# Seven half-size block products for eight in both products of an MLP, with weight sums made in DRAM

## The chip, the core and the metric

The kernel runs on one core of a Trainium2 chip. The core has a matrix engine (TensorE, PE in the profile, with PEld for its weight loads), a vector engine (VectorE, DVE), a scalar engine (ScalarE, ACT), GpSimd (POOL) and SyncE (SP). SP and POOL issue the DMAs, each in the order of its own instruction stream, and 16 DMA engines carry them. The metric is the device time of one execution in microseconds (us).

## The reference

One decoder layer in float32 on 1024 tokens of width 1024, cut here to its outline:

```python
n = rms_norm(h, ln_mix_g); proj = n @ w_in                       # q, k, v of two mixers, and gates
ya = dilated_mixture(rope(qa), rope(ka), va) @ w_branch_a        # 12 heads, windows at strides 1, 4, 16
yb = stick_breaking(qb, kb, vb) @ w_branch_b                     # 8 heads
h = h + (sigmoid(ga + b) * ya + sigmoid(gb + b) * yb) @ w_out
h = h + cross_attention(rms_norm(h), rms_norm(mem))              # 256 memory tokens
u = conv3(rms_norm(h, ln_ffn_g) @ w_up) + conv_b                 # w_up 1024 x 5632, causal, per column
h = h + (silu(u[:, :2816]) * u[:, 2816:]) @ w_down               # w_down 2816 x 1024
return rms_norm(h, ln_f_g)
```

## The kernel before

Every matrix product is made of fp32 values split in two: `split` (lines 71 to 74) lets ACT write the rounded high part `wh` and DVE the rest `wl`, and `mm3` (lines 86 to 90) issues three matmuls for each pair of 128x128 and 128x512 blocks. Raw weights come through `raw_w` (line 65, tile `wr`, two buffers), which SP loads.

The program has three parts. **Mixers**: ten pairs of heads, numbered 0 to 9. For a pair, `proj_pair` projects q, k and v (tile `mm`, or `mmv` in `v_group`); `rope` sends four DMAs `xw<-xs` on POOL (line 284) and multiplies on POOL (line 286); `k_stacks` sends the copies `kh` and `kl` on POOL (lines 245, 247); `dil_scores` multiplies q with k into `zs` (lines 254, 255) for the pairs 0 to 5. While one pair is attended, the next one is projected. **Middle**: output projection and cross-attention for two halves of 512 tokens. **MLP**: `up_pair` makes, for one half of the tokens, two gate and two value columns of 128 from eight blocks each (tile `pu`), runs the convolution (ACT line 763, DVE lines 766 and 767), silu and the product (line 770); `down_half` multiplies with w_down through `tok_gemm` (tile `mmt`, left sides `ahl`). Each half takes 44 x 8 x 3 = 1056 matmuls for w_up and 2 x 22 x 4 x 3 = 528 for w_down.

The instructions are not kept in the order in which the Python code issues them. A scheduler places each where its own timeline finds the engine free and the operands there; it keeps the order of dependent instructions only. Each engine then runs its stream in order: an instruction that waits holds up all that stand behind it on that engine, DMA issues included. DMAs of SP share eight semaphores in turn, and so do those of POOL, so that an issue waits until the eighth DMA before it on its queue has landed.

## Time and profile before

| | us |
|---|---|
| median of three runs (1783.76 to 1789.73) | 1786.36 |
| profiled execution, its own time | 1788.84 |
| its span | 1786.8 |
| PE busy in the span | 1751.7 (98%) |
| DVE, ACT, POOL busy | 1076.0, 901.9, 204.5 |
| mean granted TensorE clock | 0.996 |

The profiled execution is 2.5 us slower than the median, and 2.0 us of its time lie outside the span. A matmul of the page lasts some 390 ns from start to modelled end, but the next one starts before it ends; what a matmul costs is read from the spacing of the starts, or from a stretch in which PE does nothing else. A DMA line gives bytes and the busy share of the 16 DMA engines; "to landing" is the time from issue to the last byte.

### The profile page before, as it was taken

The numbers are of one execution on the slowest core, as the hardware profiler recorded it, in microseconds if no ns is written. First come the engines' busy times: TensorE is split into PE (matmuls) and PEld (weight loads), VectorE is DVE, ScalarE is ACT, GpSimd is POOL, SyncE is SP. The second block draws the span as 40 slices with busy tenths as digits, with TensorE's granted clock in tenths as the row PEclk, the third lists the DMA queues.
The fourth block names the chain that finished last, engine by engine and source line by source line (L and its number), as shares of the span: only waits on it lengthen the run. The fifth ranks groups of instructions, "written<-read, shape, count | busy, mean of one in ns | idle before, by whom it ended". The sixth has DMA issues, their size and how long they took to land.

```text
span 1786.8 us, 24490 instructions
## 1 busy us (share of the span) xinstructions
PE 1751.7 (98%) x8974; PEld 1441.6 (81%) x8974; DVE 1076.0 (60%) x1970; ACT 901.9 (50%) x1772; POOL 204.5 (11%) x376
## 2 busy tenths in 40 slices
...
GB/s 292 142 122 96 82 95 85 92 59 108 137 48 101 54 77 77 191 169 247 130 83 72 82 72 83 95 101 100 95 95 95 143 103 97 94 95 94 99 101 84
DMA packets 58681, 191.52 MB, mean 107 GB/s; under 512 B 10176, under 2 KB 10432, under 8 KB 58560
## 3 DMA queue, kind: packets, MB, share of 16 engines
...
## 4 chain that ended last, share of the span: by engine, by line
PE 78%; issue 11%; DMA 4%; DVE 4%; POOL 1%; ACT 1%; SPq 0%; POOLq 0%; DVEq 0%; ACTq 0%
PE pu L89 9%; PE pu L88 9%; PE pu L90 9%; PE mmt L88 7%; PE mmt L89 7%; PE mmt L90 7%; PE mm L89 4%; PE mm L88 4%; PE mm L90 4%; DMA xw<-xs 2%; PE avs L493 1%; PE mmv L88 1%; PE mmv L90 1%; PE mmv L89 1%; PE tra L486 1%
## 5 line engine op out<-in xcount | busy, mean ns | idle before, releaser
L73 DVE TENSOR_TENSOR wl<-wr,wh 128x512 fp32r<-128x512 f32 x464 | 328.3, 710 | 352.1 <-ACT wh L72 350.7
L72 ACT ACTIVATE wh<-wr 128x512 fp32r<-128x512 f32 x464 | 289.7, 626 | 468.8 <-PE pu L89 159.2
L90 PE MATMUL pu<-a2h,wl 128*128 128x512 f32 x704 | 274.9, 390 | 0.0
L89 PE MATMUL pu<-a2l,wh 128*128 128x512 f32 x704 | 274.6, 390 | 0.0
L88 PE MATMUL pu<-a2h,wh 128*128 128x512 f32 x704 | 274.4, 390 | 0.0
L88 PE MATMUL mm<-a2h,wh 128*128 128x512 f32 x640 | 253.4, 398 | 7.6 <-ACT a2h L97 7.6
L89 PE MATMUL mm<-a2l,wh 128*128 128x512 f32 x640 | 254.2, 397 | 0.0
L90 PE MATMUL mm<-a2h,wl 128*128 128x512 f32 x640 | 252.8, 397 | 0.0
L88 PEld LDWEIGHTS pu<-a2h,wh 128*128 128x128 f32 x704 | 132.2, 188 | 27.2
L90 PEld LDWEIGHTS pu<-a2h,wl 128*128 128x128 f32 x704 | 132.2, 188 | 27.2
L89 PEld LDWEIGHTS pu<-a2l,wh 128*128 128x128 f32 x704 | 132.2, 188 | 27.0
L88 PEld LDWEIGHTS mm<-a2h,wh 128*128 128x128 f32 x640 | 121.7, 190 | 31.7 <-ACT a2h L97 8.1
L89 PEld LDWEIGHTS mm<-a2l,wh 128*128 128x128 f32 x640 | 121.9, 190 | 24.1 <-issue 1.0
L90 PEld LDWEIGHTS mm<-a2h,wl 128*128 128x128 f32 x640 | 121.3, 190 | 24.6 <-issue 1.4
L89 PE MATMUL mmt<-wl,ahl 128*128 128x512 f32 x352 | 137.7, 393 | 0.0
L90 PE MATMUL mmt<-wh,ahl 128*128 128x512 f32 x352 | 136.3, 389 | 0.0
L88 PE MATMUL mmt<-wh,ahl 128*128 128x512 f32 x352 | 129.5, 392 | 0.0
L479 DVE TENSOR_TENSOR_SCAN kp<-kp 128x128 f32<-128x128 f32 (+7 forms) x64 | 86.8, 1356 | 21.5 <-ACT kp L476 21.4
L766 DVE SCALAR_TENSOR_TENSOR y<-u,vec,y 128x512 f32<-128x512 f32 x88 | 66.1, 751 | 44.0 <-ACT y L763 44.0
L367 ACT ACTIVATE sp<-sp,nm 128x128 f32<-128x128 f32 (+1 forms) x96 | 42.4, 443 | 73.4 <-DVE nm L365 73.3
L88 PEld LDWEIGHTS mmt<-wh,ahl 128*128 128x128 f32 x352 | 66.1, 188 | 15.1
L90 PEld LDWEIGHTS mmt<-wh,ahl 128*128 128x128 f32 x352 | 66.1, 188 | 14.7
...
## 6 DMA issues: line engine op xcount, KB each, us to landing
wr<-in_w_up_dram SPq DMA_DIRECT2D x88, 512.0 KB, 3.3
wr<-in_w_down_dram SPq DMA_DIRECT2D x44, 512.0 KB, 3.3
wr<-in_w_in_dram SPq DMA_DIRECT2D x37, 512.0 KB, 4.0
ga_d<-xr POOLq DMA_DIRECT2D x16, 512.0 KB, 4.4
g<-ga_d SPq DMA_DIRECT2D x16, 512.0 KB, 4.2
wr<-in_w_out_dram SPq DMA_DIRECT2D x16, 512.0 KB, 3.4
wr<-in_w_v_dram SPq DMA_DIRECT2D x12, 512.0 KB, 4.0
...
```

Of the source, the lines that this page charges most:

```text
L72: nc.scalar.activation(hi, raw, AF.Copy)
L73: nc.vector.tensor_tensor(lo, raw, f(hi), op=ALU.subtract)
L88: nc.tensor.matmul(ps, wh, rh, start=first, stop=False)
L89: nc.tensor.matmul(ps, wh, ro, start=False, stop=False)
L90: nc.tensor.matmul(ps, wo, rh, start=False, stop=last)
L367: nc.scalar.activation(sp[:, a, :n], sp[:, a, :n], AF.Exp, scale=0.125, bias=nm[:, a:a + 1], accum_out=ost[:, 130 + a:131 + a])
L479: nc.vector.tensor_tensor_scan(rev, rev, rev, 1.0, op0=ALU.mult, op1=ALU.bypass)
L486: nc.tensor.transpose(tp[:, b * P:(b + 1) * P], gg[:, (b0 + b) * P:(b0 + b + 1) * P], ident)
L493: nc.tensor.matmul(av[a * 64:(a + 1) * 64, (i % 4) * P:(i % 4 + 1) * P], st["v"][:, b, a * 64:(a + 1) * 64], ats[a][b // 4][:, (b % 4) * P ...
L766: nc.vector.scalar_tensor_tensor(y, u[:, 1:HT + 1], vec[:, cw + 1:cw + 2], y, op0=ALU.mult, op1=ALU.add)
```

## The change

Both products of the MLP are written as a 2x2 block product with seven products of blocks instead of eight (Winograd's form of Strassen's scheme). For w_up the token halves are the columns of the right side, the two halves of the 1024 inputs are its rows, and gate and value columns are the two rows of the left side; for w_down the halves are the tokens, the even and odd groups of 128 inner columns, and the two output halves.

The sums and differences that the scheme needs are made as follows. Of the **weights**: in DRAM, in `weight_sums`. For two column groups at a time, it issues four DRAM-to-DRAM copies on SP (lines 517, 518, 520, 522 of the changed file) and three adding DMAs on POOL (519, 521, 523), in a chain of seven steps in which each reads what an earlier one wrote. There are 17 such chains (11 for w_up, 6 for w_down, the last one of half the size), so 68 copies and 51 adding DMAs. `sum_step` advances the chains by one step after each second unit of the pairs 1 to 9. Of the **normalized tokens**: on DVE and ACT, in `right_sums`. Of the **activations**: on DVE, in `up_end`, from where POOL stores seven variants in DRAM (`r_d`); `down` loads them back.

A product accumulates into a PSUM bank that is read, then added to further (`pA`, `pB`, `pD`; `dA`, `dB`). The residual `h` is parked in DRAM during the MLP. For the first six column groups the two products that need only the first half of the tokens are made during cross-attention (`up_early`) and parked in DRAM too. Weights are split in one piece of 1024 columns (two buffers) where it was two of 512 (four buffers). The convolution runs over 1024 columns at a time, without the carried columns between token halves.

The diff, cut to its core ("..." marks what is left out):

```diff
+NEARLY = 6
...
+    su_d = dp.tile([NF, P, 4, HT], F32, name="su_d")
+    sd_d = dp.tile([NF // 2, P, 4, HT], F32, name="sd_d")
+    r_d = dp.tile([NF // 2, 7, P, HT], F32, name="r_d")
+    e_d = dp.tile([NEARLY, 2, P, HT], F32, name="e_d")
+    h_d = dp.tile([8, P, D], F32, name="h_d")
...
-        hi = bp.tile([P, n], F32R, tag="wh", name="wh", bufs=4)
-        lo = bp.tile([P, n], F32R, tag="wl", name="wl", bufs=4)
+        hi = bp.tile([P, n], F32R, tag="wh", name="wh", bufs=2)
+        lo = bp.tile([P, n], F32R, tag="wl", name="wl", bufs=2)
+        return split_to(hi, lo, raw)
+
+    def split_to(hi, lo, raw):
         nc.scalar.activation(hi, raw, AF.Copy)
         nc.vector.tensor_tensor(lo, raw, f(hi), op=ALU.subtract)
         return hi, lo
...
+    def weight_sums(dst, w1, w2):
+        c = slice(0, HT), slice(HT, 2 * HT)
+        add = dict(accum_op=ALU.add)
+        return [
+            lambda: nc.sync.dma_start(dst[:, :, 1], w1[:, :, c[0]]),
+            lambda: nc.sync.dma_start(dst[:, :, 2], w2[:, :, c[0]]),
+            lambda: nc.gpsimd.dma_start(dst[:, :, 1:3].rearrange("g p a c -> g p (a c)"), w2, **add),
+            lambda: nc.sync.dma_start(dst[:, :, 0], dst[:, :, 2]),
+            lambda: nc.gpsimd.dma_start(dst[:, :, 0], w1[:, :, c[0]], **add),
+            lambda: nc.sync.dma_start(dst[:, :, 3], dst[:, :, 0]),
+            lambda: nc.gpsimd.dma_start(dst[:, :, 3], w1[:, :, c[1]], **add),
+        ]
...
+    sums = []
+    for g in range(0, NF, 2):
+        sums.append(weight_sums(su_d[g:g + 2], w_up[g:g + 2], w_up[NF + g:NF + g + 2]))
+    for kg in range(0, NF // 2, 2):
+        e = min(kg + 2, NF // 2)
+        sums.append(weight_sums(sd_d[kg:e], w_down[0, kg:e], w_down[1, kg:e]))
...
+    def sum_step():
+        n = sums_n[0]
+        sums_n[0] += 1
+        for d in range(7):
+            b = n - d
+            if 0 <= b < len(sums):
+                sums[b][d]()
...
             fn(*a)
+            if p and u % 2:
+                sum_step()
...
-    def up_pair(th, fp, acts):
...
-                ps = pp.tile([P, HT], F32, tag="mm", name="pu", bufs=3)
-                feat_gemm(ps, w_up[j], n3[th])
-                u = xp.tile([P, HT + 2], F32, tag="u", name="u", bufs=2)
-                y = xp.tile([P, HT], F32, tag="y", name="y", bufs=4)
...
-                nc.scalar.activation(u[:, 2:], ps, AF.Copy)
-                cw = V_CW + 3 * j
-                nc.scalar.activation(y, ps, AF.Identity, scale=vec[:, cw + 2:cw + 3], bias=vec[:, V_CB + j:V_CB + j + 1])
-                if th == 0:
-                    nc.gpsimd.tensor_copy(carry[:, j], u[:, HT:HT + 2])
-                nc.vector.scalar_tensor_tensor(y, u[:, 1:HT + 1], vec[:, cw + 1:cw + 2], y, op0=ALU.mult, op1=ALU.add)
-                nc.vector.scalar_tensor_tensor(y, u[:, 0:HT], vec[:, cw:cw + 1], y, op0=ALU.mult, op1=ALU.add)
-                ys.append(y)
-            nc.scalar.activation(ys[0], ys[0], AF.Silu)
-            nc.vector.tensor_tensor(a2[:, e], ys[0], ys[1], op=ALU.mult)
-            acts.append(a2[:, e])
...
-    def down_half(th, acts):
...
-        for ch in range(2):
-            tok_gemm(th, ch, NF // 2, w_down, lhs, final)
...
+    def product(ps, w, r, first):
+        for kk in range(4):
+            ks = slice(kk * P, (kk + 1) * P)
+            mm3(ps, (w[0][:, ks], w[1][:, ks]), (r[0][:, kk], r[1][:, kk]), first and kk == 0, kk == 3,
+                skip_group_check=True)
...
+    def up_early(g):
+        l11, l12 = gate_weights(g)
+        pa, pb = bank("mm", 3, "pe"), bank("mm", 3, "pe")
+        p1, c11 = etile("p1"), etile("c11")
+        product(pa, l11, R["11"], True)
+        nc.scalar.activation(p1, pa, AF.Copy)
+        product(pb, l12, R["21"], True)
+        nc.vector.tensor_tensor(c11, pb, p1, op=ALU.add)
+        nc.gpsimd.dma_start(e_d[g, 0], p1)
+        nc.gpsimd.dma_start(e_d[g, 1], c11)
...
+    def right_blocks(xns):
+        hi, lo = act2()
+        R["22"], R["t1"] = (hi[:, 0:4], lo[:, 0:4]), (hi[:, 4:8], lo[:, 4:8])
+        b12 = [htile([P, 2, HT], "hu", "b12") for _ in range(2)]
+        b22 = [htile([P, 2, HT], "hy", "b22") for _ in range(2)]
+        for k in range(4):
...
+                nc.scalar.activation(b[k // 2][:, k % 2], tp, AF.Copy, scale=vec[:, V_FFN + q:V_FFN + q + 1])
+        return b12, b22
+
+    def right_sums(b12, b22):
+        for n in ("t2", "t3", "t4"):
+            R[n] = mp.tile([P, 4, HT], F32R, name=n + "h"), mp.tile([P, 4, HT], F32R, name=n + "l")
+
...
+        t1, t2 = [], []
+        for i in range(2):
+            c = slice(2 * i, 2 * i + 2)
+            a = htile([P, 2, HT], "hr", "t1f")
+            nc.vector.tensor_tensor(a, f(R["11"][0][:, c]), b12[i], op=ALU.subtract)
+            nc.vector.tensor_tensor(a, a, f(R["11"][1][:, c]), op=ALU.add)
+            t1.append(a)
+            b = htile([P, 2, HT], ("hr", "hy")[i], "t2f")
+            nc.vector.scalar_tensor_tensor(b, b22[i], -1.0, a, op0=ALU.mult, op1=ALU.subtract)
+            t2.append(b)
+            put("t2", b, c)
+        for i in range(2):
+            c = slice(2 * i, 2 * i + 2)
+            nc.vector.tensor_tensor(b12[i], b22[i], b12[i], op=ALU.subtract)
+            put("t3", b12[i], c)
+        for i in range(2):
+            put("t1", t1[i], slice(2 * i, 2 * i + 2))
+        for i in range(2):
+            put("22", b22[i], slice(2 * i, 2 * i + 2))
+        for i in range(2):
+            c = slice(2 * i, 2 * i + 2)
+            nc.vector.scalar_tensor_tensor(t2[i], t2[i], -1.0, f(R["21"][0][:, c]), op0=ALU.mult, op1=ALU.subtract)
+            nc.vector.tensor_tensor(t2[i], t2[i], f(R["21"][1][:, c]), op=ALU.subtract)
+            put("t4", t2[i], c)
+
...
+            nc.gpsimd.memset(u[n][:, 0:2], 0.0)
+        u["A"] = bank("zz", 2, "pA")
+        if g < NEARLY:
+            u["p1"] = etile("p1")
+            nc.sync.dma_start(u["p1"], e_d[g, 0])
+            nc.sync.dma_start(u["ug"][:, 2:2 + HT], e_d[g, 1])
         else:
...
+            l11, u["l12"] = gate_weights(g)
+            product(u["A"], l11, R["11"], True)
+            u["p1"] = etile("p1")
+            nc.scalar.activation(u["p1"], u["A"], AF.Copy)
+        return u
+
+    def sum_weights(g, c):
+        raw = htile([P, 2, HT], "hr", "sr")
+        nc.sync.dma_start(raw, su_d[g][:, c:c + 2])
+        hi = mp.tile([P, 2, HT], F32R, tag="mh", name="mh", bufs=2)
+        lo = mp.tile([P, 2, HT], F32R, tag="ml", name="ml", bufs=2)
+        split_to(hi, lo, raw)
+        return [(hi[:, i], lo[:, i]) for i in range(2)]
...
+    def up_middle(g, u):
+        early = g < NEARLY
+        if not early:
+            d = bank("mm", 3, "pD")
+            product(d, u["l12"], R["21"], True)
+            nc.vector.tensor_tensor(u["ug"][:, 2:2 + HT], d, u["p1"], op=ALU.add)
+        s2, s3 = sum_weights(g, 0)
+        product(u["A"], s2, R["t2"], early)
+        u["U2"] = etile("U2")
+        if early:
+            nc.vector.tensor_tensor(u["U2"], u["A"], u["p1"], op=ALU.add)
+        else:
+            nc.scalar.activation(u["U2"], u["A"], AF.Copy)
+        u["B"] = bank("tr", 2, "pB")
+        product(u["B"], s3, R["t3"], True)
+        s1, u["s4"] = sum_weights(g, 2)
+        product(u["A"], s1, R["t1"], False)
+        u4 = etile("U4")
+        if early:
+            nc.vector.tensor_tensor(u4, u["A"], u["p1"], op=ALU.add)
+        else:
+            nc.scalar.activation(u4, u["A"], AF.Copy)
+        nc.vector.tensor_tensor(u["uv"][:, 2 + HT:2 + T], u["B"], u4, op=ALU.add)
+
+    def up_end(g, u):
+        early = g < NEARLY
+        product(u["A"], u["s4"], R["22"], False)
+        c12 = u["ug"][:, 2 + HT:2 + T]
+        if early:
+            nc.vector.tensor_tensor(c12, u["A"], u["p1"], op=ALU.add)
+        else:
+            nc.scalar.activation(c12, u["A"], AF.Copy)
+        raw = bp.tile([P, HT], F32, tag="wr", name="wr", bufs=2)
+        nc.sync.dma_start(raw, w_up[NF + g][:, HT:])
+        product(u["B"], split(raw), R["t4"], False)
+        nc.vector.tensor_tensor(u["uv"][:, 2:2 + HT], u["B"], u["U2"], op=ALU.add)
...
+            nc.scalar.activation(y, x_[:, 2:2 + T], AF.Identity, scale=cw[:, c0 + 2:c0 + 3], bias=vec[:, cb:cb + 1])
+            nc.vector.scalar_tensor_tensor(y, x_[:, 1:1 + T], cw[:, c0 + 1:c0 + 2], y, op0=ALU.mult, op1=ALU.add)
+            nc.vector.scalar_tensor_tensor(y, x_[:, 0:T], cw[:, c0:c0 + 1], y, op0=ALU.mult, op1=ALU.add)
+            if not sign:
+                nc.scalar.activation(y, y, AF.Silu)
+            ys.append(y)
+        a = ys[1]
+        nc.vector.tensor_tensor(a, ys[0], a, op=ALU.mult)
...
+            nc.gpsimd.dma_start(r_d[kg, 0], a[:, :HT])
...
+        nc.vector.tensor_tensor(t[0], r11, r12, op=ALU.subtract)
...
+    def down():
+        KG = NF // 2
+        left = [lambda kg: w_down[0, kg][:, :HT], lambda kg: w_down[0, kg][:, HT:], lambda kg: sd_d[kg][:, 3],
+                lambda kg: w_down[1, kg][:, HT:], lambda kg: sd_d[kg][:, 2], lambda kg: sd_d[kg][:, 0],
+                lambda kg: sd_d[kg][:, 1]]
...
+        def run(ps, i, first):
+            for kg in range(KG):
+                raw = dn.tile([P, 2, HT], F32, tag="rl", name="rl", bufs=6)
+                nc.sync.dma_start(raw[:, 0], r_d[kg, i - 1])
+                nc.sync.dma_start(raw[:, 1], left[i - 1](kg))
+                hi = dn.tile([P, 2, HT], F32R, tag="dh", name="dh", bufs=4)
+                lo = dn.tile([P, 2, HT], F32R, tag="dl", name="dl", bufs=4)
+                split_to(hi, lo, raw)
+                for t in range(4):
+                    ts_ = slice(t * P, (t + 1) * P)
+                    mm3(ps[t], (hi[:, 0, ts_], lo[:, 0, ts_]), (hi[:, 1], lo[:, 1]), first and kg == 0, kg == KG - 1,
+                        skip_group_check=True)
...
+        def into(ps, th, ch, op, last=None):
+            for t in range(4):
+                hs = h[4 * th + t][:, ch * HT:(ch + 1) * HT]
+                nc.vector.tensor_tensor(hs, hs, ps[t], op=op)
+                if last is not None:
+                    square(4 * th + t, ch, dn.tile([P, HT + 4], F32, tag="sq", name="sq", bufs=2)[:, :HT], last)
...
+        run(A, 1, True)
...
+        B = [bank("zz", 2, "dB") for _ in range(2)] + [bank("tr", 2, "dB") for _ in range(2)]
+        run(B, 2, True)
+        into(B, 0, 0, ALU.add, 0)
+        run(A, 6, False)
+        into(A, 0, 1, ALU.subtract)
+        run(B, 7, True)
+        into(B, 1, 1, ALU.subtract)
+        run(A, 5, False)
+        into(A, 1, 1, ALU.subtract, 0)
+        run(B, 4, False)
+        into(B, 0, 1, ALU.subtract, 1)
+        out_half(0)
+        run(A, 3, False)
+        into(A, 1, 0, ALU.add, 1)
+        out_half(1)
...
-    n3 = [norm_T(0, V_FFN, True)]
+    n3 = norm_T(0, V_FFN, True)
+    R["11"], R["21"] = [tuple(x_[:, c:c + 4] for x_ in n3) for c in (0, 4)]
...
-    acts = [[], []]
-    for fp in range(NEARLY + 1):
-        up_pair(0, fp, acts[0])
+    for g in range(NEARLY // 2):
+        up_early(g)
...
-    down_half(0, acts[0])
-    for fp in range(NP_):
-        up_pair(1, fp, acts[1])
-    down_half(1, acts[1])
+    xns = normed(1)
+    for t in range(4, 8):
+        spill_h(t)
+    b12, b22 = right_blocks(xns)
+    for g in range(NEARLY // 2, NEARLY):
+        up_early(g)
...
+    right_sums(b12, b22)
+    before = None
+    for g in range(NF):
+        u = up_start(g)
+        if before is not None:
+            up_end(g - 1, before)
+        up_middle(g, u)
+        before = u
+    up_end(NF - 1, before)
+    ms.close()
+    dn = ctx.enter_context(tc.tile_pool(name="dn", bufs=1, side="right"))
+    down()
```

**SP, the first weight loads.** `wr` are weights for PE, `xk` tokens for the norm, `su_d` and `sd_d` the sums in DRAM, `rs_p` scales. Before, from the second load of `wr` after the tables:

```order
L65 DMA wr<-in_w_v_dram 128x1024
L158 DMA xk<-in_x_dram 128x1024 x3
L65 DMA wr<-in_w_v_dram 128x1024 x2
L175 DMA rs_p_653<-rs_d 128x2x1 x4
L177 DMA rs_p_654<-rs_d 64x8x1 x2
L65 DMA wr<-in_w_in_dram 128x1024 x5
```

Now, the same stretch, from the last but one first step of the chains:

```order
L517 DMA sd_d<-in_w_down_dram 256x512
L518 DMA sd_d<-in_w_down_dram 256x512
L71 DMA wr<-in_w_v_dram 128x1024
L517 DMA sd_d<-in_w_down_dram 128x512
L518 DMA sd_d<-in_w_down_dram 256x512
L518 DMA sd_d<-in_w_down_dram 128x512
L71 DMA wr<-in_w_v_dram 128x1024
L520 DMA su_d<-su_d 256x512
L71 DMA wr<-in_w_in_dram 128x1024
L520 DMA su_d<-su_d 256x512
L71 DMA wr<-in_w_in_dram 128x1024
L520 DMA su_d<-su_d 256x512 x7
```

The third load of `w_v` now stands behind 31 of the 34 copies of the first two steps, and all 68 copies stand ahead of the second pair of tables, where the code issues them between the pairs 1 and 6.

**POOL, the k copies of pair 1.** `xw` is rope's swapped copy, `kh` and `kl` are the stacked k, `o_d` attended tokens. Before:

```order
L284 DMA xw<-xs 32x1024 x4
L245 DMA kh<-kh 64x1024 x2
L247 DMA kl<-kl 64x1024
L286 TENSOR_TENSOR xw<-xw,sin 128x1024
L247 DMA kl<-kl 64x1024
L398 DMA o_d<-ost 128x132
```

Now, up to the last `kl` of pair 1:

```order
L523 DMA su_d<-in_w_up_dram 256x512 x5
L298 TENSOR_TENSOR xw<-xw,sin 128x1024
L523 DMA su_d<-in_w_up_dram 256x512
L523 DMA sd_d<-in_w_down_dram 256x512
L296 DMA xw<-xs 32x1024 x4
L257 DMA kh<-kh 64x1024
L523 DMA sd_d<-in_w_down_dram 256x512
L257 DMA kh<-kh 64x1024
L259 DMA kl<-kl 64x1024
L523 DMA sd_d<-in_w_down_dram 256x512
L259 DMA kl<-kl 64x1024
```

Ahead of that last `kl` stand all 17 adding DMAs of line 519, all 17 of line 521 and 14 of the 17 of line 523, the last step of the chains.

**DVE, the start of the MLP.** `t1f` to `t4l` are the sums of the token blocks and their low parts, `ml` the low part of summed weights, `U` a partial result. Now, ten rows from the preparation (before, DVE has weight splits and the convolution of further column groups here):

```order
L862 TENSOR_TENSOR t1f<-a2h,b_9836 128x1024
L1072 TENSOR_SCALAR ncw<-vec 128x66
L82 TENSOR_TENSOR t3l<-b_9835,t3h 128x1024
L82 TENSOR_TENSOR a2l<-b_9838,a2h 128x1024
L82 TENSOR_TENSOR t2l<-t2f,t2h 128x1024
L863 TENSOR_TENSOR t1f<-t1f,a2l 128x1024
L871 TENSOR_TENSOR b_9836<-b_9838,b_9836 128x1024
L82 TENSOR_TENSOR ml<-sr,mh 128x1024
L879 SCALAR_TENSOR_TENSOR t2f<-t2f,a2h 128x1024
L865 SCALAR_TENSOR_TENSOR t2f<-b_9838,t1f 128x1024
```

New operations of 1024 columns fill DVE between the last transposes and the first complete right side `t2` of a block product.

## Rows read from the trace of the kernel before

**Rows 1.** The page, part 1: busy us (share of the span) and instructions.
```profile
PE 1751.7 (98%) x8974; PEld 1441.6 (81%) x8974; DVE 1076.0 (60%) x1970; ACT 901.9 (50%) x1772; POOL 204.5 (11%) x376
```
**Rows 2.** Timeline of PE: start us, duration us, three matmuls in a row.
```profile
20.19 0.39 PE L89 MATMUL mm<-a2l,wh 128*128 128x512 f32 x1
20.42 0.39 PE L90 MATMUL mm<-a2h,wl 128*128 128x512 f32 x1
20.65 0.39 PE L88 MATMUL mm<-a2h,wh 128*128 128x512 f32 x1
```
**Rows 3.** Busy us by stretch (instructions); then granted clock, DMA share, GB/s.
```profile
25.00:131.00 106.00, 101.90 (x592) 86.93 (x590) 72.40 (x106) 50.10 (x100) 39.54 (x47) 1.00 0.53 148
131.00:735.00 604.00, 593.40 (x3582) 481.64 (x3580) 372.50 (x809) 310.44 (x697) 99.54 (x155) 0.99 0.31 91
1295.00:1420.00 125.00, 125.00 (x548) 102.60 (x547) 67.00 (x114) 55.88 (x107) 4.20 (x6) 1.00 0.31 100
1420.00:1655.00 235.00, 235.00 (x1039) 194.58 (x1038) 137.93 (x201) 121.44 (x201) 21.56 (x43) 1.00 0.32 104
```
**Rows 4.** Groups by line and form on PE: busy us, mean ns, idle before.
```profile
L90 PE MATMUL pu<-a2h,wl 128*128 128x512 f32 x704 | 274.9, 390 | 0.0
L89 PE MATMUL mmt<-wl,ahl 128*128 128x512 f32 x352 | 137.7, 393 | 0.0
```
**Rows 5.** DMAs from 0 to 25 us: GB/s in 40 slices, then the sum.
```profile
GB/s 0 0 27 212 242 226 154 200 252 272 311 279 406 426 419 406 377 397 419 397 420 419 393 406 416 413 413 406 396 388 395 398 423 426 413 426 420 419 420 419
DMA packets 3220, 8.53 MB, mean 341 GB/s; under 512 B 349, under 2 KB 605, under 8 KB 3220
```
**Rows 6.** DMAs from 25 to 131 us: the sum.
```profile
DMA packets 6868, 15.70 MB, mean 148 GB/s; under 512 B 3059, under 2 KB 3059, under 8 KB 6860
```
**Rows 7.** Timeline of SP's DMA issues: start us, duration us, count.
```profile
25.41 0.33 SPq L65 DMA_DIRECT2D wr<-in_w_v_dram  x1
...
41.76 3.86 SPq L65 DMA_DIRECT2D wr<-in_w_v_dram  x2
...
96.20 67.56 SPq L65 DMA_DIRECT2D wr<-in_w_in_dram  x5
```
**Rows 8.** Timeline of POOL, around the k copies of pair 1.
```profile
97.42 1.05 POOL L245 DMA_DIRECT2D kh<-kh  x2
...
106.76 0.56 POOL L247 DMA_DIRECT2D kl<-kl  x1
```
**Rows 9.** Timeline of PE, the first scores of pair 1.
```profile
130.68 0.36 PE L254 MATMUL zs<-kh,qa 128*128 128x256 f32 x1
```
**Rows 10.** Groups by line and form on DVE and ACT: busy us, mean ns.
```profile
L73 DVE TENSOR_TENSOR wl<-wr,wh 128x512 fp32r<-128x512 f32 x456 | 325.2, 715 | 352.0 <-ACT wh L72 350.7 <-PE mm L90 0.6
L767 DVE SCALAR_TENSOR_TENSOR y<-u,vec,y 128x512 f32<-128x512 f32 x88 | 66.2, 752 | 2.9
L548 DVE TENSOR_TENSOR h<-mmt,h 128x512 f32<-128x512 f32 x48 | 32.6, 686 | 14.3 <-PE mmt L90 14.2
L580 DVE TENSOR_TENSOR yl<-wr,yh 128x1024 fp32r<-128x1024 f32 x6 | 7.3, 1225 | 15.0 <-ACT yh L579 14.8
L579 ACT ACTIVATE yh<-wr 128x1024 fp32r<-128x1024 f32 x6 | 6.4, 1060 | 16.7 <-DMA wr<-yt_d 16.7
L763 ACT ACTIVATE y<-pu,vec 128x512 f32<-128x512 f32 x88 | 68.0, 772 | 0.0
L761 ACT ACTIVATE u<-pu 128x512 f32<-128x512 f32 x88 | 51.2, 582 | 0.0
```
**Rows 11.** DMA issues by line: count, KB each, median us to landing.
```profile
wr<-in_w_up_dram SPq DMA_DIRECT2D x88, 512.0 KB, 3.3
o_d<-ost POOLq DMA_DIRECT2D x32, 33.0 KB, 1.8
```

171 lines of the change are left out of this document (111 added, 60 removed).

## The prediction

> **What bounds the kernel now.** The page's first part shows PE busy for 98% of the span, DVE for 60% and ACT for 50% [rows 1]. Durations on PE mislead: the timeline shows matmuls of 0.39 us that start 0.227 us apart [rows 2], so neighbours overlap. The price of a matmul is the spacing. The table by stretch says it for the MLP: in the stretch from 1295 to 1420 us, when w_down is multiplied, 548 matmuls take 125 us (0.228 us each), and from 1420 to 1655 us, w_up for the second half, 1039 take 235 us (0.226), both at a granted clock of 1.00 with DVE at 54 to 59% [rows 3]. So the MLP is paced by PE, and each matmul taken away there is worth 0.227 us, not the 390 ns of the grouped rows [rows 4]. The mixers are paced by PE too, but by a small margin: from 25 to 131 us PE is busy 102 of 106 us, and there POOL and the DMA engines (0.53) are busiest [rows 3]. Two more things are to be seen in the early stretch: SP issues the weights just ahead of their use (two at 41.8 us, five from 96 to 164 us) [rows 7], and POOL sends the k of pair 1 at 97 to 107 us [rows 8] for scores that start at 130.7 us [rows 9]. Nothing there has slack beyond some 25 us.
>
> **What the change removes.** The w_up product has 3 x 704 = 2112 matmuls, the w_down product 3 x 352 = 1056 [rows 4]. Seven instead of eight block products take an eighth away: 264 + 132 = 396. At 0.227 us that is **-90 us**, all on the path, as nothing else ends there.
>
> **What it adds in the MLP.** A 1024-column TENSOR_TENSOR takes DVE 1.225 us, a 512-column one out of PSUM 0.686; a SCALAR_TENSOR_TENSOR of 512 takes 0.752, so at most 1.5 for 1024 [rows 10]. `right_sums` is 18 plain and 4 three-operand operations of 1024: 18 x 1.225 + 4 x 1.5 = 28 us. A column group g below 6 needs, on DVE, five additions out of PSUM (3.4), two splits of summed weights (2.5) and half a split (0.7), four convolution steps (6.0), the product (1.2) and on average two differences (1.4): 15.2 us, while its five block products of 12 matmuls give PE 5 x 12 x 0.227 = 13.6 us. For the six groups DVE needs 28 + 91 = 119 us and PE 82. Of the 37 us, the last convolution and product (9 us) need not be done before PE goes on, and some 3 us of sums run beside the last transposes: **+25 us**, between 5 (`up_early` covers more of the sums) and 40 (none of it is covered). From group 6 on DVE has 15 us, ACT some 11 (three splits at 1.06, one at 0.6, four copies at 0.58, two convolution starts of at most 1.54 and silu) and PE 7 x 12 x 0.227 = 19 us: covered. In `down`, each step has 12 matmuls (2.7 us) against one split of 1.06 on ACT and 1.225 on DVE: covered; if that cover were gone, it would be 0 to 1 us for each of 77 steps. The pools are changed twice; the first change lies under the sums, the second exposes a load, a high part and a low part: 3.3 [rows 11] + 1.06 + 1.2 = **+6 us** (0 to 12). Last results and the longer final multiplications: **+4 us** (0 to 8). The MLP as a whole: -90 + 25 + 6 + 4 = **-55 us** (-85 to -30). The parked tiles, the r_d stores and loads and the wider weight splits lie beside PE work of 14 to 19 us a group and go at nothing; without that cover they cost a load each, 3.3 us.
>
> **What the sums move: the queues.** This decides the sign. The scheduler has pulled the 68 copies and 51 adding DMAs to the first place where SP and POOL are free. On SP, the third weight load of `w_v` stands behind 31 copies; on POOL, the rope and k copies stand among the adding DMAs. Both engines issue in order, and each issue waits for the eighth one before it, so SP and POOL go on at the pace at which the DMA engines carry the sums. The last point that holds PE is the last `kl` of pair 1 on POOL. Ahead of it are adding DMAs of 17.3 MB (step 3), 8.65 MB (step 5) and 14 x 0.52 = 7.3 MB (step 7), and, as each step needs the one before, copies of 17.3 + 8.65 + 7.3 MB: 33.3 MB copied and 33.3 MB added. Behind it waits `zs` of pair 1 on PE, and behind that the whole program. In the kernel before, that matmul starts at 131 us [rows 9]; by then 8.5 MB had moved by 25 us [rows 5] and 15.7 MB from 25 to 131 us [rows 6]. The sums begin at about 25 us, when SP has issued its second `w_v` load [rows 7].
>
> How fast? No row shows a DRAM-to-DRAM copy or an adding DMA. The nearest is the stretch 0 to 25 us, with loads queued up without a gap: slices of 390 to 426 GB/s [rows 5], I take 420. A load touches DRAM once per byte. A copy there touches it twice; an addition reads two operands and writes one, three times. The bounds are to count every byte once (15.7 + 66.6 = 82 MB, 196 us, the point at 221 us) and every touch (15.7 + 2 x 33.3 + 3 x 33.3 = 182 MB, 434 us, the point at 459 us). I take the upper one, since both ends of these transfers lie in the place that the 420 GB/s came from. The delay is then 459 - 131 = **+328 us**. What PE does before that point it did before, too, so the wait is not won back: afterwards PE has 593 us of work in 604 [rows 3].
>
> The Trainium skill ("DMA: Bandwidth & Descriptors", section "Latency and other measured facts") gives 207 to 214 GB/s for copies between HBM tensors; by it the 33.3 MB of copies alone would take some 159 us, an estimate, which is also what two touches at 420 GB/s give, and no run here shows it yet.
>
> **Sum.** 1788.8 for the profiled execution, + 328 - 55 = 2062; less the 2.5 us by which that execution is above the median: **2059 us**.
>
> **Rivals.**
> *Reads set the pace.* A copy counts once, an addition twice (two reads), writes run beside: 15.7 + 33.3 + 66.6 = 115.6 MB at 420 GB/s, 275 us; the point at 300 us, delay 169, time 1900. For it speaks that a load is also a read with a write (into SBUF) that costs no extra at 420 GB/s [rows 5]; against it, that here the writes go to DRAM as well. The Trainium skill ("Collectives: The Full Stack", section "The bandwidth ceiling: the fold count and why AG ≠ RS ≠ AR") has a reduction run at half a copy's rate because it reads two sources; that is this case, and no row here shows it.
> *Every byte counts once.* The point at 221 us, delay 90, time 1786 + 90 - 55 = 1821. Against it speaks that an addition must read its target.
> *The sums hide beside the mixers, faster.* Over 25 to 735 us the DMA engines are busy a third of the time [rows 3], so there is room for 66.6 MB twice over if the queues let other work pass. Then only the MLP counts: 1786 - 55 = 1731. It decides below a delay of 55 us: the point must be reached by 186 us, 82 MB in 161 us, 511 GB/s. The trace has no slice above 426.
> *Rows go out one by one.* If an adding DMA carries one row at a time on each engine and each takes the 1.8 us of the smallest stores [rows 11]: 4224 + 4224 + 3584 rows over 16 engines, 752 in turn, 1354 us; time about 3000. For it: the additions read, add and write back the same place. Against it: nothing in the trace shows such a lack of overlap.
>
> **How the numbers follow.** All touches 0.50; reads only 0.25; bytes once 0.08; hidden 0.07; row by row 0.10. The likeliest gives 2059. The range takes in the first three cases: from 1815 up to 2059 plus 25 for a poorer MLP and 95 for a rate that is a fifth lower over the 434 us, 2180. A measurement of this kernel tells 0.3% from no change. Faster by more than that 0.07 (the hidden case), within 0.01, slower 0.92.
>
> **What would show it.** In the profile after: a stretch between 30 and some 400 us in which PE is mostly idle and the DMA engines are busy for nine tenths or more, with SP's loads of `wr` waiting for DMAs on `su_d` and `sd_d`, and POOL's `kl` of pair 1 sent at about 450 us. The scores of pair 1 start there instead of at 131 us, and the distance from them to the end shrinks by some 55 us, from 1656 to about 1600. In the MLP 1848 matmuls on w_up's product and 924 on w_down's, with a gap of 15 to 35 us before and during the first groups, ended by DVE. I am wrong if PE stays above 90% from 131 us on (the hidden case), if the waiting is ended by compute and not by DMAs, or if the sums take over half a millisecond.

## The result, and the profile after

The changed kernel takes **1989.93 us** (median of four runs, 1987.86 to 1990.65), the kernel before beside it 1786.69: ratio **1.1135, 95% interval 1.1115 to 1.1156**. The forecast was 2059, in the range 1815 to 2180: slower, as forecast, but by 203 us and not by 273. Of the profiled execution the span is 1988.2 us. The page's busy times and slices, where [rows 1] showed a PE at 98%:

```profile
PE 1692.6 (85%) x8578; PEld 1384.4 (70%) x8578; DVE 1093.1 (55%) x1723; ACT 833.2 (42%) x1410; POOL 272.3 (14%) x444
...
PE   7102554799999899999999999879999999959997
...
DMA  9999999633322512212555223245544344276664
```

Each slice is some 50 us. In the first seven the DMA line stands at 9, and from the second to the seventh PE is idle for about half of the time or more. The table by stretch (busy time with instructions for PE, PEld, DVE, ACT, POOL; then granted clock, DMA share, GB/s) gives the numbers; before, PE was busy for 102 of the 106 us from 25 to 131 us and for 593 of the next 604 [rows 3]:

```profile
25.00:60.00 35.00, 34.34 (x194) 29.70 (x192) 2.45 (x2) 5.72 (x9) 4.87 (x7) 1.00 1.05 272
60.00:100.00 40.00, 0.00 (x0) 0.00 (x0) 0.00 (x0) 2.30 (x4) 3.55 (x4) 0.52 1.03 276
100.00:150.00 50.00, 1.97 (x8) 1.57 (x8) 5.29 (x11) 2.30 (x4) 7.14 (x7) 0.50 1.09 203
...
60.00:350.00 290.00, 89.61 (x448) 72.97 (x448) 46.14 (x85) 40.16 (x80) 67.60 (x80) 0.64 1.07 250
```

From 60 to 350 us PE works for 90 of 290 us, with the DMA share at 1.07 and 203 to 276 GB/s in slices of 40 or 50 us. What PE waits for there, from the waits of 0 to 420 us (who waited, for whom, us in all, times, longest):

```profile
PE mmv L98 <- ACT wh L81: 63.9, 2, 61.5
PE trr L125 <- POOL rs L111: 57.9, 1, 57.9
PE mm L98 <- ACT wh L81: 37.6, 2, 31.2
PE mm L98 <- ACT xs L237: 29.8, 2, 25.0
```

`wh` is the high part of weights whose load stood behind the copies on SP; `rs` is an operation of POOL itself (the power in the norm's scale), which stood behind adding DMAs. The second is a wait that the forecast did not name, of the kind it did. The end of the blockage, in the order of time: SP's third load of `w_v`, the second `kh` copy and the last `kl` copy of pair 1 on POOL, and the first scores of pair 1 on PE.

```profile
149.01 5.34 SPq L71 DMA_DIRECT2D wr<-in_w_v_dram  x1
...
340.13 0.53 POOL L257 DMA_DIRECT2D kh<-kh  x1 [4.31 <-DMA su_d<-in_w_up_dram]
...
347.34 0.54 POOL L259 DMA_DIRECT2D kl<-kl  x1 [0.58 <-PE avd L398]
...
350.62 0.58 PE L266 MATMUL zs<-kh,qa 128*128 128x256 f32 x1 [3.82 <-DMA kh<-kh]
```

By the profile it is a `kh` copy that releases these scores and the next ones at 355.10 us, and not the `kl` copy behind it that the forecast named; both stand among the adding DMAs. The answers of before are POOL's `kl` at 106.76 us [rows 8] and `zs` at 130.68 us [rows 9]: the scores start 220 us later. From there to the end it is 1637.6 us instead of 1656.1, so the rest won 18.5 us, not 55. The first matmul of the branch products (`pbr`) shows the same in one number, 744.3 us before and 967.9 after, +223.6.

**The MLP.** The stretches from the last query projection of cross-attention (1013 us before, 1237 after) to the end hold 774 us before and 751 after. PE works 763 us of the one and 689 of the other, so the products lost 74 us of PE time, and 51 us came back as idle time:

```profile
1237.00:1280.00 43.00, 36.29 (x188) 29.21 (x186) 26.70 (x58) 20.89 (x50) 3.30 (x6) 1.00 0.29 98
1280.00:1325.00 45.00, 41.82 (x188) 33.39 (x188) 22.37 (x36) 19.45 (x37) 8.34 (x13) 0.96 0.35 123
1325.00:1340.00 15.00, 5.18 (x16) 3.49 (x17) 15.00 (x16) 9.03 (x11) 0.64 (x2) 0.60 0.31 99
1340.00:1360.00 20.00, 17.36 (x68) 12.82 (x67) 16.08 (x17) 7.09 (x7) 0.10 (x1) 0.96 0.42 138
...
1700.00:1733.00 33.00, 31.63 (x136) 25.20 (x136) 21.66 (x23) 14.89 (x18) 4.73 (x12) 1.00 0.28 96
1733.00:1765.00 32.00, 6.82 (x24) 5.00 (x23) 12.82 (x15) 7.26 (x7) 6.98 (x13) 0.62 0.69 234
...
1975.00:1988.00 13.00, 0.00 (x0) 0.00 (x0) 7.07 (x14) 4.22 (x8) 4.44 (x4) 0.69 0.43 162
```

Before, all of the 11 us of idle time lie behind the last matmul. Now it is 10 us beside cross-attention (1237 to 1325), 12 at the first column groups (1325 to 1360, DVE busy for all of the first 15), 27 around the first product of `down` (25.2 of them in one wait), and 13 at the end.

### The profile page after: what moved, and what is told of

The parts are those of the page before. It is cut to its first block, busy times and chain, and to the rows that moved or that the text cites. A ratio compares the mean times of both kernels' runs of the same rounds, so it can differ in the third digit from the quotient of the medians.

```text
span 1988.2 us, 23423 instructions
## 1 busy us (share of the span) xinstructions
PE 1692.6 (85%) x8578; PEld 1384.4 (70%) x8578; DVE 1093.1 (55%) x1723; ACT 833.2 (42%) x1410; POOL 272.3 (14%) x444
## 4 chain that ended last, share of the span: by engine, by line
PE 67%; DMA 17%; issue 9%; SPq 3%; DVE 3%; ACT 1%; POOL 1%; POOLq 0%; ACTq 0%; DVEq 0%
DMA sd_d<-in_w_down_dram 5%; PE mm L98 5%; PE mm L99 5%; PE mm L100 5%; PE pA L98 4%; PE pA L100 4%; PE pA L99 4%; PE dA L98 2%; PE dA L100 2%; PE dA L99 2%; DMA su_d<-in_w_up_dram 2%; PE pB L99 2%; PE pB L100 2%; PE pB L98 2%; DMA xk<-in_x_dram 2%
## 5 line engine op out<-in xcount | busy, mean ns | idle before, releaser
L82 DVE TENSOR_TENSOR wl<-wr,wh 128x1024 fp32r<-128x1024 f32 (+2 forms) x141 | 159.5, 1132 | 223.8 <-ACT wh L81 222.7
L81 ACT ACTIVATE wh<-wr 128x1024 fp32r<-128x1024 f32 (+2 forms) x141 | 138.1, 981 | 275.5 <-DMA wr<-in_w_v_dram 86.2
L99 PE MATMUL mm<-a2l,wh 128*128 128x512 f32 x592 | 236.7, 400 | 0.0
L82 DVE TENSOR_TENSOR dl<-rl,dh 128x1024 fp32r<-128x1024 f32 x77 | 94.3, 1224 | 99.0 <-ACT dh L81 98.3
L81 ACT ACTIVATE dh<-rl 128x1024 fp32r<-128x1024 f32 x77 | 81.6, 1060 | 129.0 <-DMA rl<-in_w_down_dram 43.2
L98 PE MATMUL mmv<-wh,a2h 128*128 128x256 f32 x192 | 56.9, 298 | 66.0 <-ACT wh L81 63.9
L98 PE MATMUL dA<-dh 128*128 128x512 f32 x176 | 66.0, 398 | 25.2 <-ACT dh L81 25.2
L98 PE MATMUL pA<-a2h,mh 128*128 128x512 f32 x176 | 69.8, 397 | 1.8 <-ACT U L925 0.7
L99 PE MATMUL pA<-a2l,mh 128*128 128x512 f32 x176 | 69.5, 395 | 0.0
L100 PE MATMUL pA<-a2h,ml 128*128 128x512 f32 x176 | 69.5, 395 | 0.0
L99 PE MATMUL dA<-dl,dh 128*128 128x512 f32 x176 | 69.4, 395 | 0.0
```

The source lines that it names most:

```text
L81: nc.scalar.activation(hi, raw, AF.Copy)
L82: nc.vector.tensor_tensor(lo, raw, f(hi), op=ALU.subtract)
L98: nc.tensor.matmul(ps, wh, rh, start=first, stop=False, **kw)
L99: nc.tensor.matmul(ps, wh, ro, start=False, stop=False, **kw)
L100: nc.tensor.matmul(ps, wo, rh, start=False, stop=last, **kw)
```

## The experiments

Three questions: are the sums the whole of the loss (and what is the MLP worth); at what rate do the DMA engines carry them; and is it their bytes or their place that costs?

### 1. Without the sums

```diff
-            if p and u % 2:
-                sum_step()
...
-        nc.sync.dma_start(raw, su_d[g][:, c:c + 2])
+        nc.sync.dma_start(raw, w_up[g if c == 0 else NF + g].rearrange("p (a c) -> p a c", a=2))
...
-... sd_d[kg][:, 3], w_down[1, kg][:, HT:], sd_d[kg][:, 2], sd_d[kg][:, 0], sd_d[kg][:, 1]
+... w_down[1, kg][:, :HT], w_down[1, kg][:, HT:], w_down[0, kg][:, HT:], w_down[1, kg][:, :HT], w_down[0, kg][:, :HT]
```

> The changed kernel without the weight sums: no copies and no adding DMAs, and the products that need a sum of weights read a plain block of the same size instead (so this kernel leaves the sums out of the computation). Theory 'the queues': the whole loss of 223 us up to the end of the mixers is the sums', and the seven products are worth what the second half of the trace shows, 22 us; time 1764 (1755 to 1775), the first branch products (pbr) at 744 us as before. Rival 'the seven products slow the rest as well' (wider weight splits, two buffers instead of four, in the mixers): the branch products start 10 us or more later than 744 and the time is 1775 or above.

Measured: **1767.67 us**, 0.988 of before (0.9863 to 0.9897), `pbr` at 745.2 us. Both numbers are the first theory's. So the sums cost 1989.9 - 1767.7 = **222 us**, all of it ahead of the branch products, and the seven products are worth 22 us as they stand (1789.6 for the kernel before beside it).

### 2. What the DMA engines can carry

The transfers alone, behind the last store of the kernel before:

```diff
+    for g in range(0, NF, 2):
+        for i in range(2):
+            cps.append(after_(nc.sync.dma_start(su_d[g:g + 2, :, i], w_up[g + NF * i:g + NF * i + 2][:, :, 0:HT]), *last_out))
+    for g in range(0, NF, 2):
+        after_(nc.gpsimd.dma_start(su_d[g:g + 2, :, 0:2]..., w_up[NF + g:NF + g + 2], accum_op=ALU.add), *cps)
```

> The kernel before, and behind its last store 22 DRAM-to-DRAM copies of 512 KB on SP and then, when all have landed, 11 adding DMAs of 1 MB on POOL, with nothing beside them: 11.5 MB each. By all touches at 420 GB/s (my prediction): copies 55 us (210 GB/s), additions 82 us (140 GB/s), time about 1925. By reads alone: copies 27 us, additions 55 us, time about 1870. By the one rate of 255 GB/s that the changed kernel showed for the mixture: 45 us each, time about 1880.

Measured: 1898.37 us in one run. The table by stretch, first while only copies run, then while only additions run:

```profile
1790.00:1820.00 30.00, 0.00 (x0) 0.00 (x0) 0.00 (x0) 0.00 (x0) 0.00 (x0) 0.50 1.03 324
1840.00:1880.00 40.00, 0.00 (x0) 0.00 (x0) 0.00 (x0) 0.00 (x0) 1.76 (x2) 0.50 1.06 198
```

**Copies run at 324 GB/s, additions at 198**, with nothing beside them and the engines full, in the steady part of each; over the whole of each kind, its start and end included, it is 304 (1786 to 1822 us) and 185 (1826 to 1888). None of the three expectations had this pair. A copy costs 1.3 times what a load at 420 costs [rows 5], not twice; an addition 2.1 times, not three times.

Then the same inside the changed kernel, with every DMA in its place on its queue. First the additions as plain copies:

```diff
-        add = dict(accum_op=ALU.add)
+        add = dict()
```

> The changed kernel with its 51 adding DMAs as plain copies of the same bytes in the same places of the same queues (so the sums are not formed). By the rates of the isolated run (copies 324 GB/s, additions 198): 33.3 MB more at 324 instead of 198 takes 65 us from the wait, the last kl of pair 1 at about 280 us, time about 1925. By one rate for both: no change, 1990. By touches, two for a copy and three for an addition: a fifth of 322 us less, time about 1930. So this run tells the one rate from the other two.

Then without them:

```diff
-            lambda: nc.gpsimd.dma_start(dst[:, :, 1:3].rearrange("g p a c -> g p (a c)"), w2, **add),
+            lambda: None,
...
-            lambda: nc.gpsimd.dma_start(dst[:, :, 0], w1[:, :, c[0]], **add),
+            lambda: None,
...
-            lambda: nc.gpsimd.dma_start(dst[:, :, 3], w1[:, :, c[1]], **add),
+            lambda: None,
```

> The changed kernel without its 51 adding DMAs, the 68 copies left where they are (the sums are not formed). By the isolated rate: 34.6 MB at 324 GB/s are 107 us of the DMA engines from 20 us on, beside 16 MB of other loads; the third load of w_v stands behind 31 copies and comes at about 75 us instead of 42; the delay is 30 to 60 us and the time 1798 to 1828. By two touches each at 420 GB/s (210 GB/s): 165 us of copies, delay about 90, time about 1858. If SP's order alone made the loss in the changed kernel, the time stays near 1990.

Measured, one run each: **1930.33** and **1840.53 us**. With plain copies the last `kl` of pair 1 leaves POOL at 287.86 us (forecast about 280, in the changed kernel 347.34):

```profile
287.86 0.52 POOL L259 DMA_DIRECT2D kl<-kl  x1 [0.64 <-DMA xw<-xs]
```

The first run excludes one rate for both kinds (1990). The second lies between the first two of its expectations (1798 to 1828, and 1858), and excludes the third, that the order on SP alone made the whole loss (1990). Against the DMA time of the sums at the isolated rates, the three kernels stand in a line:

| | DMA time of the sums | us above the kernel without sums |
|---|---|---|
| copies only | 34.6 / 0.324 = 107 | 73 |
| all as copies | 69.2 / 0.324 = 214 | 163 |
| as changed | 107 + 34.6 / 0.198 = 282 | 222 |

All but 34 to 60 us of the DMA time shows on PE. With copies alone PE still waits 27 us for the weights of `w_v` and 25 for those of `w_in`, so copies at the head of SP's queue hold PE up without any adding DMA on POOL:

```profile
PE mmv L98 <- ACT wh L81: 27.1, 1, 27.1
PE mm L98 <- ACT wh L81: 25.2, 2, 17.3
```

### 3. The sums in other places

All 119 DMAs stay. Each is pinned behind one that the surrounding work issues on the same queue, so that the scheduler can't pull it to the start:

```diff
+    flat = [sums[n - d][d] for n in range(len(sums) + 6) for d in range(7) if 0 <= n - d < len(sums)]
...
+            inst = flat.pop(0)().ins
+            tc.add_manual_dep(inst, last[eng].ins.name, mybir.DependencyInfo(
+                mybir.DependencyClass.NoSync, mybir.DependencyReason.DATA), reason="pace")
...
-            if p and u % 2:
-                sum_step()
+            if p:
+                sum_step(1 if p < NA else 2.5)
```

> The changed kernel with all its sums, but each of the 119 DMAs pinned on its queue behind a DMA that the mixers issue at that point (a weight load on SP, a k copy or a token store on POOL), one after each unit of the pairs 1 to 5 and two or three after each unit of the pairs 6 to 9. Theory 'the queues': the bytes are harmless, the order was not; time as without sums, 1764 (1755 to 1785), no stretch with DMA at 0.9 or more for over 50 us. Rival 'the bytes': 69 MB beside the mixers delay their loads wherever they stand; at the 255 GB/s that the changed kernel reached they take 270 us of the DMA engines, and a third of that shows: 1800 to 1860.

And with the first product of `down` in tiles of the weight pool:

```diff
+            raw = bp.tile([P, 1024], F32, tag="wr", name="wr", bufs=2)
+            nc.sync.dma_start(raw[:, :HT], r_d[kg, 0])
+            nc.sync.dma_start(raw[:, HT:], w_down[0, kg][:, :HT])
+            hi, lo = split(raw)
...
-        run(A, 1, True)
```

> As the paced kernel, and the first of the seven products of w_down takes its tiles from the pool that the weight splits use (wr, wh, wl), so that it need not wait for the pool of the w_up part to be given back. Theory: the wait of 25 us before the first dA goes and nothing comes in its place, 25 to 28 us less than the paced kernel: about 1738 (1730 to 1758). Rival: the wait moves to the second product, which needs the new pool: the gain is under 10 us.

Measured: **1842.03** and **1818.67 us**. The first edit brought back 148 of the 222 us; the other 74 fell to the rival. The second is worth 23.4 us by the medians, of which 18 lie at its place: PE's wait before the first `dA` is 24.7 us in the paced kernel and 6.5 us, in three pieces, in the other, and the distance from the last `pA` to the end falls from 252.6 to 234.4. The rest lies in the mixers (819.7 to 811.4 us at the branch products), where both programs have the same lines; why is not known. So the theory (25 to 28 us, nothing in the place of the wait) holds for the better part, and its time of 1738 was missed with that of the paced kernel, from which it was counted. The table by stretch of the paced kernel shows where the 74 us went: PE loses most where the DMA engines are at 0.95.

```profile
131.00:347.00 216.00, 203.42 (x1148) 163.06 (x1149) 102.58 (x254) 96.15 (x250) 73.34 (x102) 0.95 0.69 163
347.00:540.00 193.00, 155.06 (x906) 126.39 (x904) 89.73 (x231) 71.41 (x148) 40.19 (x60) 0.91 0.95 223
540.00:735.00 195.00, 191.30 (x1103) 153.13 (x1104) 128.96 (x234) 100.55 (x189) 27.41 (x38) 0.98 0.65 154
```

Next, thinner, and from here on with the early start of `down` in every kernel: so many DMAs behind each weight load (`raw_w`; the rate is 1.2 in the mixers and 0.6 in the middle), and the rest after each `up_middle`.

```diff
+        if rate[0]:
+            step[0](rate[0])
...
+        sum_step(1.5)
```

> All sums, with the first dA product taken from the other pool, and the 119 DMAs spread thinner: one or so behind each weight load from pair 2 to the end of cross-attention, then one or two for each column group of the w_up part, so that the last chains end inside the MLP. Theory 'density': in the paced kernel the 75 us were lost where the DMA engines were over 0.9 busy (347 to 540 us); without such a stretch the sums cost little, and the time is that of the kernel without sums less the 23 us of the earlier start of w_down: 1744, with some loss 1744 to 1765. Rival 'every adding DMA costs the mixers something' (waits behind it on POOL or slower loads, in proportion to the bytes): the loss stays near 60 us, about 1800.

> As the spread kernel, with eight column groups prepared during cross-attention instead of six (NEARLY = 8), four before its second output product and four after. Theory: the 10 us in which PE idles beside the cross-attention of the second half, and part of the 12 us at the first groups, come from too little matrix work to lay beside them; 5 to 12 us less than the spread kernel. Rival: two more groups with five additions out of PSUM each make DVE the bound for longer: no change or 3 to 5 us more.

> The spread kernel again, with other places: half a DMA of the sums behind each weight load of the pairs 2 to 5, 1.6 behind each one of the pairs 6 to 9 (where the spread kernel lost nothing, 347 to 740 us), none in the stretch of the branch products (740 to 880 us, where it lost 34 of its 55 us at a DMA share of 0.89), 0.6 in the rest of the middle and 1.8 for each column group. Theory 'it is the stages that load much themselves': the loss shrinks to 10 to 25 us, time 1755 to 1770. Rival 'the bytes cost the same everywhere': the loss stays near 55 us, 1800.

> The second spread kernel with its one fault mended: there, ten adding DMAs were pinned behind the last token store of the mixers, and eight of them left POOL in one burst at 739 to 743 us, just ahead of the branch products, which then waited for weights (DMA share 1.03 to 1.07 from 740 to 800 us). Now adding DMAs may also follow the gate stores, and no sums are issued from the end of the mixers to the second output product. Theory 'it is bursts, not bytes': the 34 us lost at the branch products shrink below 8, the kernel takes 1752 to 1765. Rival 'the bytes': the loss reappears in the stage that now carries them (pairs 6 to 9, or the w_up part), time 1780 to 1800.

Measured: **1798.68, 1799.52, 1800.81 and 1799.61 us**; each time the rival. `NEARLY = 8` changed nothing that can be told in the time; the two stages from `pq` to the last `pA` are 3.6 us shorter in its trace than in the spread kernel's, less than the 5 to 12 of its theory. Three different placings gave one time, which looked like a price per byte wherever the bytes stand. The lengths of the stages say otherwise (us from the trace; the first column is the start of `pbr`, the branch products; the others are the distances between first starts, to `pq`, the query projection of cross-attention, and to `pe`, the products of `up_early`; then to the last start of `pA` on its first line, and to the end of the span):

| | to pbr | to pq | to pe | to last pA | to the end |
|---|---|---|---|---|---|
| changed kernel | 967.9 | 135.8 | 134.9 | 494.7 | 254.9 |
| without sums | 745.2 | 137.1 | 134.9 | 497.3 | 252.3 |
| paced | 819.7 | 137.9 | 134.8 | 497.2 | 252.6 |
| paced, early down | 811.4 | 138.7 | 134.9 | 496.1 | 234.4 |
| spread | 761.6 | 161.9 | 137.4 | 501.7 | 233.3 |
| second spread | 757.2 | 158.7 | 137.4 | 507.8 | 240.8 |
| third spread | 757.5 | 148.9 | 134.7 | 504.2 | 256.4 |
| last spread (below) | 750.0 | 138.4 | 134.9 | 507.1 | 236.7 |
| sums of w_up on POOL (below) | 750.4 | 144.9 | 134.9 | 528.2 | 234.6 |

The loss moves from stage to stage, and in these traces a burst stands ahead of it. In the spread kernel, eight adding DMAs left POOL from 741.17 to 745.65 us; in the second spread, eight left within 4.4 us behind the last token store, just ahead of the branch products:

```profile
738.05 0.54 POOL L515 DMA_DIRECT2D yt_d<-ye  x1 [3.87 <-DVE ye L514]
738.59 0.97 POOL L527 DMA_DIRECT2D su_d<-in_w_up_dram  x1
...
742.98 2.90 POOL L523 DMA_DIRECT2D su_d<-in_w_up_dram  x1
```

and in the stretch behind them PE worked for 9.43 of 20 us, where the kernel without sums (second line) works for 19.22:

```profile
740.00:760.00 20.00, 9.43 (x35) 7.36 (x35) 3.47 (x4) 1.90 (x2) 6.46 (x8) 0.74 1.03 198
740.00:760.00 20.00, 19.22 (x81) 14.81 (x81) 13.03 (x18) 4.76 (x6) 0.53 (x1) 1.00 0.58 182
```

In the third spread, four of them left at 744 to 760 us, and 13 DMAs stood behind the w_up part in the program (256.4 us to the end instead of 234). The last spread takes these away and lays more of the sums into the mixers: 1.4 behind each weight load of the pairs 2 to 5, 2.5 in the pairs 6 to 9, none behind the last nine gates, 1.3 from the cross-attention of the first half on, 1.8 for each column group.

> The spread kernel a last time: in the third spread kernel 13 of the 119 DMAs were left over at the end of the w_up part and ran in one burst beside the first dA product (16 us of waits), and four adding DMAs left POOL at 744 to 760 us, ahead of the branch products. Now more of the sums stand in the mixers (1.4 behind each weight load of the pairs 2 to 5, 2.5 in the pairs 6 to 9, none behind the last nine gates), none between the last gates and the second half of the middle, 1.3 there, and 1.8 for each column group, all done before w_down starts. Theory 'bursts': no stretch loses over 10 us to the kernel without sums, 1762 to 1780. Rival 'the bytes cost some 40 to 55 us wherever they stand': 1785 to 1800.

Measured: **1767.84 us, 0.9882 of the kernel before (0.9863 to 0.9900)**. It has all the sums, moves the same 307 MB as the changed kernel, and beats both that and the kernel before. Its stretches:

```profile
131.00:735.00 604.00, 588.47 (x3548) 476.77 (x3547) 360.12 (x757) 301.35 (x648) 120.46 (x176) 0.99 0.59 150
735.00:880.00 145.00, 141.81 (x678) 117.80 (x678) 87.82 (x136) 61.45 (x90) 14.53 (x24) 1.00 0.63 198
```

With 65 of the 119 DMAs in the mixers at a DMA share of 0.59, PE works for 588 of 604 us (before: 593 [rows 3]). Against an estimate of 1767.7 - 18.2 = 1749.5 for the kernel without sums and with the early start of `down`, 18 us are left of what the sums cost, most of them in the w_up part (507 instead of 497 us; the wait for its first summed weights is 12.9 us instead of 7.0) and ahead of the branch products (750 instead of 745). Of the 21 us by which it beats the kernel before, the early start makes up some 18 by the same estimate. That bursts cost more than the same bytes spread out is argued from these stretches: places and rates changed together in each run, and none moved a burst alone.

### 4. The sums of w_up on POOL

```diff
+        nc.sync.dma_start(a, w_up[g].rearrange("p (a c) -> p a c", a=2))
+        nc.sync.dma_start(b, w_up[NF + g].rearrange("p (a c) -> p a c", a=2))
+        for o, i in ((b[:, 1], b[:, 0]), (b[:, 0], a[:, 0]), (a[:, 0], b[:, 1]), (a[:, 1], a[:, 0])):
+            nc.gpsimd.tensor_tensor(o, o, i, op=ALU.add)
```

> The sums of w_up are made by POOL in SBUF: both weight tiles of a column group are loaded, and four additions of 512 columns in place make the four sums; only the six chains of w_down stay in DRAM, behind the weight loads of the pairs 6 to 9; the first dA product is taken from the other pool. POOL's row for a 1024-column product is 2.66 us, so four additions of 512 take some 5.5 us of 17.5 us for a group. Theory: 23 MB of copies and 23 MB of additions are gone, the rest hides: 1744 to 1755. Rival 'POOL and DVE disturb each other' or POOL's sums come too late for PE: each group is longer by 1 us or more, 1770 and above.

Measured: **1797.32 us**, the rival's: the w_up part takes 31 us longer. Where it loses them, the table by stretch shows: the first groups and the rest of the w_up part of this kernel, then the rest of that part in the kernel without sums. The waits are those of 1117 to 1250 us.

```profile
1118.00:1250.00 132.00, 93.87 (x374) 72.99 (x373) 110.04 (x102) 48.77 (x49) 61.06 (x56) 0.84 0.39 128
1250.00:1561.00 311.00, 311.00 (x1352) 253.47 (x1351) 257.26 (x227) 147.94 (x175) 148.35 (x152) 1.00 0.44 146
```

```profile
1160.00:1515.00 355.00, 353.63 (x1537) 288.04 (x1535) 257.63 (x275) 165.34 (x192) 42.58 (x112) 1.00 0.44 146
```

```profile
PE pA L101 <- ACT mh L84: 28.7, 3, 26.6
PE pA L101 <- DVE U L957: 8.0, 5, 2.3
```

So of the rival's two reasons it is mainly the second: the sums come too late for PE, and only at the start. One wait of 26.6 us for the first sums (7.0 in the kernel without sums) and five waits for DVE, 8.0 us together, stand ahead of 1250 us. Behind it PE never idles, and a matmul costs 0.230 us as without sums, so no later group is longer.

POOL and DVE do slow each other, but PE doesn't see it there. The groups of that stretch, first of this kernel (POOL's additions, DVE's convolution), then of the kernel without sums (instruction counts, busy time and mean ns of one), and two times four additions on POOL:

```profile
L928 POOL TENSOR_TENSOR sr<-sr 128x512 f32<-128x512 f32 x78 | 146.6, 1879 | 83.9 <-DMA sr<-in_w_up_dram 72.5 <-DVE ml L85 5.1 <-ACT y L979 1.1
...
L981 DVE SCALAR_TENSOR_TENSOR y<-ug,vec,y 128x1024 f32<-128x1024 f32 x20 | 38.4, 1919 | 0.3
```

```profile
L954 DVE SCALAR_TENSOR_TENSOR y<-ug,vec,y 128x1024 f32<-128x1024 f32 x21 | 26.9, 1281 | 0.3
```

```profile
1152.16 5.38 POOL L928 TENSOR_TENSOR sr<-sr 128x512 f32<-128x512 f32 x4 [5.94 <-DMA sr<-in_w_up_dram]
...
1312.60 7.47 POOL L928 TENSOR_TENSOR sr<-sr 128x512 f32<-128x512 f32 x4 [5.10 <-DVE ml L85]
```

Beside a DVE that is idle for most of the time the four take 5.38 us, 1.34 each, which is the half of 2.66 that was expected; beside the convolution they take 7.47, and the mean of all is 1.88. DVE's three-operand instruction takes 1.92 us there instead of 1.28.

## Why the prediction was right in sign and 69 us off

**The sign and the mechanism: right.** The sums stand at the head of two queues that issue in order, everything behind them waits, and the wait is not won back. The kernel without sums has none of it, and its mixers run as before (745.2 us to the branch products; before 744.3). The rival "hidden" falls, as do "row by row" (the additions ran at 198 GB/s) and "every byte counts once" (the point at 221 us; it was reached at 347).

**The size of the wait: the step that failed is "I take the upper one".** The forecast gave the 15.7 MB of loads, 33.3 MB of copies and 33.3 MB of additions 434 us, with two and three touches of DRAM at 420 GB/s; the point was reached at 347 us, 322 us after the start at 25. By the isolated rates it would be 15.7 / 0.42 + 33.3 / 0.324 + 33.3 / 0.198 = 37 + 103 + 168 = 308 us, and by the rates over the whole of each kind (304 and 185) 37 + 110 + 180 = 327; the 322 lie between. Copies were priced at 210 GB/s instead of 324, additions at 140 instead of 198. The rival "reads set the pace" (275 us, the point at 300, time 1900) missed the point by 47 us, the forecast by 112; there it was the better one, with half the chance, and an addition at half the rate of a load (210) is its term and nearly what was measured. A price per touch fails for a further reason: the memory counter shows one read and one write for a copy and for an addition alike (last section), and yet the addition takes 1.6 times as long. The two bounds held the truth, and no row of the trace of before shows a transfer of either kind.

**Luck.** The two large errors have opposite signs: the wait was forecast 108 us too long (328, measured 220) and the gain of the MLP 33 us too large. With the MLP's term right the forecast would have been 2092, over 100 us off; and the rival's 1900, nearer at the point, is further off in the time. In the range, a rate that is a fifth lower over 434 us would add 108 us, not 95; nothing hangs on it.

The Trainium skill ("DMA: Bandwidth & Descriptors", section "Latency and other measured facts") gives 207 and 214 GB/s for copies between HBM tensors with rows of 16 KiB, at row pitches of 512 KiB and of 4 MiB with 4 KiB of padding; the rows here are of another layout, the trace gives 324, and the measurement decides. The Trainium skill ("Collectives: The Full Stack", section "The bandwidth ceiling: the fold count and why AG ≠ RS ≠ AR") has a reduction at half a copy's rate, for two source reads, in a ring of cores and not in a DMA of one core; the rows give 198 to 324, 0.61.

**The MLP: -55 was forecast, -22 measured (1767.7 to 1789.6 beside it).** By terms, from the stretches above:

| term | forecast | measured |
|---|---|---|
| 396 matmuls less | -90 | -74 |
| first column groups, DVE | +25 (5 to 40) | +12 |
| around the first product of `down` | +6 (0 to 12) | +27 |
| beside cross-attention | 0 | +10 |
| end | +4 (0 to 8) | +2 |

The *start of `down`* is the term that was mis-sized most. It counted the load, the high part and the low part. It left out that the new pool takes the place of the old one, so that the first load waits for the last reader of the last old tile: the last matmul of w_up starts at 1736.6, the convolution and the four differences of the last group take DVE until 1745.3, the last one is stored by POOL, that store must land, and only then SP may load. The rows in the order of time, and SP's wait:

```profile
1744.65 0.68 DVE L977 SCALAR_TENSOR_TENSOR ts<-ts,y 128x512 f32<-128x512 f32 x1
...
1746.90 0.54 POOL L978 DMA_DIRECT2D r_d<-ts  x1
...
1754.86 0.33 SPq L998 DMA_DIRECT2D rl<-r_d  x1
...
1761.05 1.06 ACT L81 ACTIVATE dh<-rl 128x1024 fp32r<-128x1024 f32 x1 [20.67 <-DMA rl<-in_w_down_dram]
...
1762.16 2.07 PE L98 MATMUL dA<-dh 128*128 128x512 f32 x4 [25.18 <-ACT dh L81]
```

```profile
SPq L998 <- DMA r_d<-ts: 58.1, 1, 58.1
```

The paced kernel with other tiles for that product shows the cause: the wait falls from 24.7 to 6.5 us, and the distance from the last `pA` to the end from 252.6 to 234.4.

The *first column groups* came out in the lower half of their range: DVE is busy without a gap from 1322 to 1350 us, as forecast, but it has begun on the sums while `up_early` still feeds PE. The gap is below the 15 to 35 us that were named as a sign, and DVE does not end its longest wait: those 7.7 us end with ACT's high part of the first summed weights, whose load SP issued at 1330.16 us and which landed at 1334.06, a load that the forecast did not price. The *10 us beside cross-attention* were not in the sum at all: before, PE idles nowhere from 1013 to 1775 us; now 72 matmuls of `up_early` stand ahead of the second half's output product and 72 behind it, where 288 of `up_pair` stood ahead of it. That this is the reason is not shown: eight groups instead of six did not bring the time down. The *matmuls* gave 16 us less than 90. Some of it can be read: w_up now runs at 300 us for 1306 matmuls, 0.230 us each instead of 0.226 [rows 3] (6 us in 1704), and the stretches after the two gaps, at a granted clock of 0.60 to 0.96, take 84 and 173 matmuls at 0.24 to 0.27 us each (5 us more). The rest stays open.
